# Two attention layers on TensorE: heads in pairs on the halves of the array, output with features on partitions

## The chip, the cores and the metric

The kernel runs on one core of one Trainium2 chip. The core has a matrix engine (TensorE, "PE"; its weight loads are shown apart as "PEld"), a vector engine (VectorE, "DVE"), a scalar engine (ScalarE, "ACT"), GpSimd ("POOL") and a queue for transfers (SyncE, "SP"). Each takes its instructions in order; they wait for each other by semaphores. The metric is the device time in microseconds, the median of several runs. Lower is better.

## What is computed

A hybrid network of four layers on a sequence of 256 tokens with 1024 features, in float32. Each layer is a SwiGLU block, a mixer and a second SwiGLU block, each followed by a weighted residual and a layer norm. The mixers are a state-space layer (layers 0 and 3), "fox" attention (layer 1: 16 heads of 64 features, causal, with a forget gate) and "moba" attention (layer 2, which for 256 tokens in one block of 256 is plain causal attention). What the change touches is, for each head:

```python
logits = einsum('bhqd,bhkd->bhqk', q, k) * 64 ** -0.5      # fox: + cum[q] - cum[k], summed log gates
logits = where(kpos <= qpos, logits, -inf)
p = softmax(logits, axis=-1)
o = einsum('bhqk,bhkd->bhqd', p, v)                         # then o @ w_out
```

## The kernel before, in words

The 256 tokens are two halves of 128, t = 0 and t = 1. All of a half's activations lie with its tokens on partitions, and are turned (features on partitions) by PE transposes to be a matmul's stationary operand. The weights are streamed once, in pieces of 128 x 2048 float32 (1 MB); each piece is split by ACT (`wh`, line 123) and DVE (`wl`, line 124) into two float32r parts, and every product with weights is three matmuls, high by high, high by low and low by high (lines 148 to 150). Half 1 follows half 0 by two pieces (`LAG`), so the two halves' work is interleaved, and a scheduler of the language that knows data dependencies and a cost of each instruction sets the final order on each engine.

An attention layer takes 16 pieces in the order of `ATT_ORDER`: for each of four groups of four heads one piece V (values) and two pieces Q (queries and keys), then four pieces O (the output projection, `down`). After a piece, stages are emitted by the table `post`. With q the second Q piece of group g:

- `stage_v` copies the values from PSUM to `kv`; `stage_q` (at q) copies queries and keys to SBUF (line 624), transposes them on PE, and writes the transposed queries, times 1/8, to `qz` (lines 627, 628) and the transposed keys to `kT` (line 629). After the transposes two heads lie on the two halves of the partitions, 64 features each. `qz` has a slot of 128 x 128 per head, whose other 64 partitions are zero: POOL cleared the tile (line 618). So a head's score matmul works on all 128 rows, and half of them meet zeros.
- `stage_s` (at q + 1) makes scores in a transposing bank `T()`: a bf16 matmul adds the causal mask (`mlo`, lines 643, 660), fox adds its gate rows by a selector (`sel`, line 654), and line 657 is queries by keys. t = 0 has 128 keys per head and all four heads in one bank; t = 1 has 256 keys (those of t = 0 and its own) and two heads per bank, one bank after the other. DVE takes the maximum of each row (line 662), ACT the exponential with its sum (line 667), DVE the reciprocal (line 670).
- `att` (at q + 2) transposes the probabilities on PE, copies them out (lines 687, 689) and multiplies: the transposed probabilities (128 keys x 128 queries) are stationary, 64 columns of values move (lines 695, 699, 700). The output has queries on partitions. DVE multiplies it by the reciprocals (line 702).
- `stage_a` (at q + 3) transposes that output on PE, two transposes of 128 columns, and splits it into `ah` and `al` for the output projection (`act_split`).

PSUM has two banks for `T()` (all transposes and scores), two for `G()` (the attention output among others) and four for accumulators. These matmuls of scores and values are in float32.

Of the kernel before, what the change touches and what calls it, by code (L numbers as in the profile page):

```python
# [49 lines left out]
def build(tc, x, wst, ln_g, ln_b, sm_dt, sm_rows, sm_conv, sm_nw, fx_f, fx_b, out, plan=None):  # L50
# [33 lines left out]
    K = {}  # L84
# [504 lines left out]
    def attn(st, kind, j):  # L589
# [27 lines left out]
        qz = spool.tile([128, 4, 128], F32, name="qz", tag="xD", bufs=2)  # L617
        nc.gpsimd.memset(qz, 0.0)
# [3 lines left out]
        def stage_q(g):  # L622
            qk = tmp(512, "t2", 4)
            nc.scalar.activation(qk, bank.pop(g), AF.Copy)
            tp = transposes(qk, 4).rearrange("p (a b) -> p a b", a=4)
            kT = kv[g][:, 0:256].rearrange("p (a b) -> p a b", a=2)
            nc.scalar.activation(qz[0:64, 0::2], tp[0:64, 0:2], AF.Copy, scale=0.125)
            nc.vector.tensor_scalar_mul(qz[64:128, 1::2], tp[64:128, 0:2], 0.125)
            nc.scalar.activation(kT, tp[:, 2:4], AF.Copy)
            if t == 0:  # L630
                s.kT[g] = kT

        def stage_s(g):
            kT = kv[g][:, 0:256].rearrange("p (a b) -> p a b", a=2)
            own = d.rows if fox else None
            rs = spool.tile([128, 12], F32, name="rs", bufs=4)
            nh = 4 if t == 0 else 2
            pt = []
            for b in range(4 // nh):
                tp = T()  # L640
                if t == 0:
                    Sv = tp.rearrange("p (h k) -> p h k", h=4)
                    nc.tensor.matmul(Sv, K["mlo"], rep4(4), start=True, stop=True, skip_group_check=True)
                    parts = [(kT, 0, own)]
                else:
                    Sv = tp.rearrange("p (h k) -> p h k", h=2)
                    parts = [(s.kT[g], 0, s.toend if fox else None), (kT, 128, own)]
                begun = t == 0
                for hh in range(nh):
                    h = b * nh + hh  # L650
                    for kt, off, rows in parts:
                        o = Sv[:, hh, off:off + 128]
                        if fox:
                            nc.tensor.matmul(o, sel(g * 4 + h), rows, start=not begun, stop=False,
                                             skip_group_check=True)
                            begun = True
                        nc.tensor.matmul(o, qz[:, h], kt[:, h // 2], start=not begun, stop=True, skip_group_check=True)  # L657
                        begun = True
                if t == 1:
                    nc.tensor.matmul(Sv[:, :, 128:256], K["mlo"], rep4(2), start=False, stop=True,  # L660
                                     skip_group_check=True)
                nc.vector.tensor_reduce(rs[:, b * nh:(b + 1) * nh], Sv, axis=AX.X, op=ALU.max, negate=True)
                p = tmp(512, "mt", 5)
                pv = p.rearrange("p (h k) -> p h k", h=nh)
                for hh in range(nh):
                    h = b * nh + hh
                    nc.scalar.activation(pv[:, hh], Sv[:, hh], AF.Exp, bias=rs[:, h:h + 1],
                                         accum_out=rs[:, 4 + h:5 + h])
                pt.append(p)
            nc.vector.reciprocal(rs[:, 8:12], rs[:, 4:8])  # L670
            ps_[g] = (pt, rs)
# [8 lines left out]
        def att(g):  # L680
            pt, rs = ps_.pop(g)
            pT = []
            for p in pt:
                tp = transposes(p, 4)
                e = tmp(512, "mt", 5)
                if t == 0:
                    nc.vector.tensor_copy(e, tp)
                else:
                    nc.scalar.activation(e, tp, AF.Copy)
                pT.append(e)  # L690
            o = G()
            for h in range(4):
                c64 = slice(h * 64, h * 64 + 64)
                if t == 0:
                    nc.tensor.matmul(o[:, c64], pT[0][:, h * 128:(h + 1) * 128], vs[g][:, c64], start=True, stop=True)
                else:
                    e = pT[h // 2]
                    b = (h % 2) * 256
                    nc.tensor.matmul(o[:, c64], e[:, b:b + 128], s.v[g][:, c64], start=True, stop=False)
                    nc.tensor.matmul(o[:, c64], e[:, b + 128:b + 256], vs[g][:, c64], start=False, stop=True)  # L700
            on = tmp(256, "t1", 5)
            nc.vector.tensor_mul(on.rearrange("p (a b) -> p a b", a=4),
                                 o[:, :256].rearrange("p (a b) -> p a b", a=4),
                                 rs[:, 8:12].unsqueeze(2).to_broadcast([128, 4, 64]))
            ons[g] = on

        ons = {}

        def stage_a(g):
            ahs[g] = act_split(ons.pop(g), 2)[0]  # L710
# [12 lines left out]
        for g in range(ATT_G):  # L723
# [5 lines left out]
            at(q + 3, stage_a, g)  # L729
# [201 lines left out]
```

## Time and profile before

| | |
|---|---|
| median of 3 runs | 2160.16 us (2158.58 to 2160.63) |
| profiled execution | 2158.25 us, its span 2156.1 us |
| PE busy | 2122.0 us (98%) |
| PEld busy | 1768.2 us (82%) |
| DVE busy | 1486.4 us (69%) |
| ACT busy | 1125.5 us (52%) |
| POOL busy | 477.6 us (22%) |

The span runs from the first to the last instruction of the profiled execution. Busy time of PE is a sum of records whose ends are modelled and which overlap in the pipe, so the spacing of starts says more than a record's length. A form such as "128\*128 128x64" gives the rows and columns of the array that a matmul uses, and then the operand that moves, as partitions x columns. The fox layer lies at about 757 to 897 us and the moba layer at about 1280 to 1403 us. "idle before <-" names what ended an engine's idle time.

### The profile page before, as it was taken

To read this page: it belongs to the slowest core of one execution; us is meant where nothing else is said; L and a number is where in the kernel's file an instruction comes from. 1 tells how busy PE (TensorE), PEld (TensorE's weight loads), DVE (VectorE), ACT (ScalarE), POOL (GpSimd) and SP (SyncE) were. 2 spreads that over 40 slices of the span, in tenths; PEclk is the share of its full clock that TensorE was granted. 3 is DMA by queue.
4 is the path that set the end of the run, shared out by engine and by line. 5 is a ranking of instruction groups with operands and counts; after the bars stand their busy time and mean duration, and the time that the engine had idled before them with its cause. 6 is when DMAs were issued, how large, how long until landed. Compare 5 with 4: busy or idle time off the path is not lost.

```text
span 2156.1 us, 29943 instructions
## 1 busy us (share of the span) xinstructions
PE 2122.0 (98%) x10370; PEld 1768.2 (82%) x10370; DVE 1486.4 (69%) x2959; ACT 1125.5 (52%) x2314; POOL 477.6 (22%) x862
## 2 busy tenths in 40 slices
PE   8999999999999999999999999999999999999998
PEld 6888878788888888888888888888888888788887
DVE  6657999855765674665575574666575679998655
ACT  6444776544444555444544455544454447665442
POOL 2331000233143200043233300033323310001431
PEclk9999999999999999999999999999999999999999
DMA  9775544676586643476666654376767665556772
GB/s 316 229 230 187 191 173 153 225 232 227 193 255 226 218 158 118 137 237 226 220 226 228 226 199 136 131 220 227 226 224 236 221 205 180 162 179 207 235 226 94
DMA packets 225927, 438.81 MB, mean 204 GB/s; under 512 B 20464, under 2 KB 20976, under 8 KB 225776
## 3 DMA queue, kind: packets, MB, share of 16 engines
q1 hardware_dynamic: 197616, 394.92, 55.1%
q0 software_dynamic: 28160, 41.99, 7.0%
q8 instruction: 81, 1.33, 0.3%
q14 instruction: 70, 0.57, 0.1%
HBM read 414.74 MB, written 22.09 MB: 203 GB/s over the span
## 4 chain that ended last, share of the span: by engine, by line
PE 93%; DVE 3%; ACT 1%; DMA 1%; issue 0%; POOL 0%; SPq 0%; DVEq 0%; ACTq 0%
PE gu L148 15%; PE gu L150 15%; PE gu L149 15%; PE acc L150 9%; PE acc L148 9%; PE acc L149 9%; PE ga L150 4%; PE ga L149 4%; PE ga L148 4%; PE tp L158 3%; PE gu L512 1%; DMA raw<-in_w_dram 1%; PE tp L657 1%; DVE wl L124 1%; DVE mt L502 1%
## 5 line engine op out<-in xcount | busy, mean ns | idle before, releaser
L124 DVE TENSOR_TENSOR wl<-raw,wh 128x512 fp32r<-128x512 f32 x1408 | 887.7, 683 | 361.8 <-ACT wh L123 360.2
L123 ACT ACTIVATE wh<-raw 128x512 fp32r<-128x512 f32 x1408 | 777.0, 621 | 528.0 <-PE gu L150 222.4
L148 PE MATMUL gu<-wh,xh 128*128 128x512 f32 (+1 forms) x1600 | 620.6, 388 | 7.1 <-ACT t L519 2.7
L150 PE MATMUL gu<-wh,xl 128*128 128x512 f32 (+1 forms) x1600 | 617.8, 387 | 0.9 <-DVE xl L124 0.9
L149 PE MATMUL gu<-wl,xh 128*128 128x512 f32 (+1 forms) x1600 | 617.4, 386 | 0.0
L246 POOL DMA_DIRECT2D aT<-turn x640 | 348.3, 551 | 503.4 <-issue 301.9
L148 PEld LDWEIGHTS gu<-wh,xh 128*128 128x128 f32 x1600 | 301.1, 188 | 69.7 <-ACT t L519 3.1
L150 PE MATMUL acc<-wh,al 128*128 128x512 f32 x896 | 353.5, 395 | 0.0
L149 PE MATMUL acc<-wl,ah 128*128 128x512 f32 x896 | 352.5, 393 | 0.0
L148 PE MATMUL acc<-wh,ah 128*128 128x512 f32 x896 | 351.5, 393 | 0.0
L150 PEld LDWEIGHTS gu<-wh,xl 128*128 128x128 f32 x1600 | 300.9, 188 | 61.6 <-DVE xl L124 2.1
L149 PEld LDWEIGHTS gu<-wl,xh 128*128 128x128 f32 x1600 | 301.2, 188 | 59.4 <-issue 0.5
L272 DVE TENSOR_TENSOR t<-t,gu 128x256 f32<-128x256 f32 x176 | 73.5, 418 | 192.5 <-ACT t L270 192.5
L270 ACT ACTIVATE t<-gu 128x256 f32<-128x256 f32 x176 | 67.5, 383 | 260.3 <-PE gu L150 239.5
L150 PEld LDWEIGHTS acc<-wh,al 128*128 128x128 f32 x896 | 168.4, 188 | 36.8 <-DVE al L124 1.9
L149 PEld LDWEIGHTS acc<-wl,ah 128*128 128x128 f32 x896 | 168.5, 188 | 34.4 <-issue 1.0
L148 PEld LDWEIGHTS acc<-wh,ah 128*128 128x128 f32 x896 | 168.5, 188 | 33.6
L148 PE MATMUL ga<-wh,xh 128*128 128x512 f32 (+1 forms) x448 | 159.6, 358 | 1.4 <-ACT xh L123 1.4
L242 POOL DMA_DIRECT2D turn<-tb x160 | 90.3, 565 | 318.6 <-DVE tb L240 297.7
L150 PE MATMUL ga<-wh,xl 128*128 128x512 f32 (+1 forms) x448 | 157.0, 351 | 0.1
L149 PE MATMUL ga<-wl,xh 128*128 128x512 f32 (+1 forms) x448 | 156.1, 349 | 0.0
L190 POOL TENSOR_TENSOR rstd<-ve,mhalf 128x1 f32<-128x1 f32 x24 | 22.6, 942 | 369.9 <-DVE ve L188 369.9
(179 smaller groups left out, 1707.0 us busy)
## 6 DMA issues: line engine op xcount, KB each, us to landing
raw<-in_w_dram SPq DMA_DIRECT2D x351, 1024.0 KB, 5.6
turn<-tb POOLq DMA_DIRECT2D x160, 128.0 KB, 3.4
aT<-turn POOLq DMA_DIRECT2D x640, 32.0 KB, 4.1
mt<-cums SPq DMA_DIRECT2D x32, 256.0 KB, 4.9
gb<-in_ln_g_dram SPq DMA_DIRECT2D x12, 512.0 KB, 4.6
gb<-in_ln_b_dram SPq DMA_DIRECT2D x12, 512.0 KB, 6.1
nw<-in_sm_nw_dram SPq DMA_DIRECT2D x8, 256.0 KB, 5.6
h<-in_x_dram SPq DMA_DIRECT2D x4, 256.0 KB, 4.3
```

What stands on the lines that cost most here:

```text
L123: a = nc.scalar.activation(wh, raw, AF.Copy)
L124: return a, nc.vector.tensor_sub(wl, raw, wh.bitcast(F32))
L148: nc.tensor.matmul(o, xh, wh, start=start, stop=False)
L149: nc.tensor.matmul(o, xh, wl, start=False, stop=False)
L150: nc.tensor.matmul(o, xl, wh, start=False, stop=stop)
L158: nc.tensor.transpose(tp[:, j * 128:(j + 1) * 128], src[:, j * 128:(j + 1) * 128], ident)
L190: nc.gpsimd.tensor_tensor(rstd, ve, mhalf, op=ALU.pow)
L242: nc.gpsimd.dma_start(dr, b.rearrange("p q k t -> p (q k t)"))
L246: nc.gpsimd.dma_start(aT[32 * q:32 * q + 32].rearrange("p i k t -> p i (k t)"), dv[q])
L270: nc.scalar.activation(sg, gu[:, :256], AF.Silu)
L272: nc.vector.tensor_mul(a, sg, gu[:, 256:])
L502: nc.vector.tensor_scalar(e[:, h], e[:, h], d.ncum[:, h0 + h:h0 + h + 1], 0.0, op0=ALU.add, op1=ALU.min)
```

## The change

- The queries are no longer padded: `qT` holds two pairs of heads, 128 partitions x 2 x 128, written by one DVE instruction. The cleared tile is gone. A head's score matmul takes 64 partitions, `qT[half, i]` by `kt[half, i]`, where half is rows 0 to 63 or 64 to 127; the two heads of a pair write to two banks, `Sv[0]` and `Sv[1]`, and follow each other in program order.
- Both banks are taken at the start for either half of the tokens. The mask comes first in each bank, then fox's selector matmuls, then all scores.
- The probabilities are multiplied by the reciprocals in SBUF, before they are transposed.
- In `att` the values, 128 keys x 64 features, are stationary and the transposed probabilities, 128 columns, move. A pair's outputs go to partitions 0 to 63 and 64 to 127 of one bank, so features are on partitions, and `ah` and `al` are split straight from PSUM. `stage_a` with its two transposes is gone. `h_at` gives a head's place in the order of t = 0, where the heads of a bank lie beside each other.

```diff
@@ -614,8 +614,7 @@
                 foxs[key].kT, foxs[key].v = {}, {}
             s = foxs[key]
         ahs, ps_, vs, kv = {}, {}, {}, {}
-        qz = spool.tile([128, 4, 128], F32, name="qz", tag="xD", bufs=2)
-        nc.gpsimd.memset(qz, 0.0)
+        qT = spool.tile([128, 2, 128], F32, name="qT", tag="xD", bufs=2)
 
         bank = {}
 
@@ -624,51 +623,48 @@
             nc.scalar.activation(qk, bank.pop(g), AF.Copy)
             tp = transposes(qk, 4).rearrange("p (a b) -> p a b", a=4)
             kT = kv[g][:, 0:256].rearrange("p (a b) -> p a b", a=2)
-            nc.scalar.activation(qz[0:64, 0::2], tp[0:64, 0:2], AF.Copy, scale=0.125)
-            nc.vector.tensor_scalar_mul(qz[64:128, 1::2], tp[64:128, 0:2], 0.125)
+            nc.vector.tensor_scalar_mul(qT, tp[:, 0:2], 0.125)
             nc.scalar.activation(kT, tp[:, 2:4], AF.Copy)
             if t == 0:
                 s.kT[g] = kT
 
         def stage_s(g):
+
             kT = kv[g][:, 0:256].rearrange("p (a b) -> p a b", a=2)
             own = d.rows if fox else None
             rs = spool.tile([128, 12], F32, name="rs", bufs=4)
-            nh = 4 if t == 0 else 2
-            pt = []
-            for b in range(4 // nh):
-                tp = T()
-                if t == 0:
-                    Sv = tp.rearrange("p (h k) -> p h k", h=4)
-                    nc.tensor.matmul(Sv, K["mlo"], rep4(4), start=True, stop=True, skip_group_check=True)
-                    parts = [(kT, 0, own)]
-                else:
-                    Sv = tp.rearrange("p (h k) -> p h k", h=2)
-                    parts = [(s.kT[g], 0, s.toend if fox else None), (kT, 128, own)]
-                begun = t == 0
-                for hh in range(nh):
-                    h = b * nh + hh
-                    for kt, off, rows in parts:
-                        o = Sv[:, hh, off:off + 128]
-                        if fox:
-                            nc.tensor.matmul(o, sel(g * 4 + h), rows, start=not begun, stop=False,
-                                             skip_group_check=True)
-                            begun = True
-                        nc.tensor.matmul(o, qz[:, h], kt[:, h // 2], start=not begun, stop=True, skip_group_check=True)
-                        begun = True
-                if t == 1:
-                    nc.tensor.matmul(Sv[:, :, 128:256], K["mlo"], rep4(2), start=False, stop=True,
-                                     skip_group_check=True)
-                nc.vector.tensor_reduce(rs[:, b * nh:(b + 1) * nh], Sv, axis=AX.X, op=ALU.max, negate=True)
-                p = tmp(512, "mt", 5)
+            parts = [(kT, 0, own)] if t == 0 else [(s.kT[g], 0, s.toend if fox else None), (kT, 128, own)]
+            nk = 128 * len(parts)
+            Sv = [T()[:, :2 * nk].rearrange("p (h k) -> p h k", h=2) for b in range(2)]
+            for b in range(2):
+                nc.tensor.matmul(Sv[b][:, :, nk - 128:nk], K["mlo"], rep4(2), start=True, stop=True,
+                                 skip_group_check=True)
+                if fox:
+                    for i in range(2):
+                        for kt, off, rows in parts:
+                            nc.tensor.matmul(Sv[b][:, i, off:off + 128], sel(g * 4 + 2 * i + b), rows, start=False,
+                                             stop=True, skip_group_check=True)
+            for i in range(2):
+                for kt, off, rows in parts:
+                    for b in range(2):
+                        half = slice(64 * b, 64 * b + 64)
+                        nc.tensor.matmul(Sv[b][:, i, off:off + 128], qT[half, i], kt[half, i], start=False, stop=True,
+                                         skip_group_check=True)
+            pt = [tmp(512, "mt", 5) for b in range(1 + t)]
+            for b in range(2):
+                nc.vector.tensor_reduce(rs[:, 2 * b:2 * b + 2], Sv[b], axis=AX.X, op=ALU.max, negate=True)
+                pv = pt[b if t else 0][:, 0 if t else b * 256:][:, :2 * nk].rearrange("p (h k) -> p h k", h=2)
+                for i in range(2):
+                    n = 2 * b + i
+                    nc.scalar.activation(pv[:, i], Sv[b][:, i], AF.Exp, bias=rs[:, n:n + 1],
+                                         accum_out=rs[:, 4 + n:5 + n])
+            nc.vector.reciprocal(rs[:, 8:12], rs[:, 4:8])
+            nh = 4 // (1 + t)
+            for n, p in enumerate(pt):
                 pv = p.rearrange("p (h k) -> p h k", h=nh)
-                for hh in range(nh):
-                    h = b * nh + hh
-                    nc.scalar.activation(pv[:, hh], Sv[:, hh], AF.Exp, bias=rs[:, h:h + 1],
-                                         accum_out=rs[:, 4 + h:5 + h])
-                pt.append(p)
-            nc.vector.reciprocal(rs[:, 8:12], rs[:, 4:8])
-            ps_[g] = (pt, rs)
+                nc.vector.tensor_mul(pv, pv, rs[:, 8 + n * nh:8 + (n + 1) * nh].unsqueeze(2).to_broadcast(
+                    [128, nh, nk]))
+            ps_[g] = pt
 
         def stage_v(g):
             kv[g] = tmp(512, "xe" if t == 0 and g % 2 else f"xdt{t}", 1 + t)
@@ -678,9 +674,9 @@
                 s.v[g] = vs[g]
 
         def att(g):
-            pt, rs = ps_.pop(g)
+
             pT = []
-            for p in pt:
+            for p in ps_.pop(g):
                 tp = transposes(p, 4)
                 e = tmp(512, "mt", 5)
                 if t == 0:
@@ -689,25 +685,22 @@
                     nc.scalar.activation(e, tp, AF.Copy)
                 pT.append(e)
             o = G()
-            for h in range(4):
-                c64 = slice(h * 64, h * 64 + 64)
-                if t == 0:
-                    nc.tensor.matmul(o[:, c64], pT[0][:, h * 128:(h + 1) * 128], vs[g][:, c64], start=True, stop=True)
-                else:
-                    e = pT[h // 2]
-                    b = (h % 2) * 256
-                    nc.tensor.matmul(o[:, c64], e[:, b:b + 128], s.v[g][:, c64], start=True, stop=False)
-                    nc.tensor.matmul(o[:, c64], e[:, b + 128:b + 256], vs[g][:, c64], start=False, stop=True)
-            on = tmp(256, "t1", 5)
-            nc.vector.tensor_mul(on.rearrange("p (a b) -> p a b", a=4),
-                                 o[:, :256].rearrange("p (a b) -> p a b", a=4),
-                                 rs[:, 8:12].unsqueeze(2).to_broadcast([128, 4, 64]))
-            ons[g] = on
-
-        ons = {}
-
-        def stage_a(g):
-            ahs[g] = act_split(ons.pop(g), 2)[0]
+            blocks = [vs[g]] if t == 0 else [s.v[g], vs[g]]
+            for i in range(2):
+                for kb, v in enumerate(blocks):
+                    for b in range(2):
+                        h = 2 * i + b
+                        e = pT[b][:, (2 * i + kb) * 128:] if t else pT[0][:, h_at(h) * 128:]
+                        nc.tensor.matmul(o[64 * b:64 * b + 64, i * 128:i * 128 + 128], v[:, h * 64:h * 64 + 64],
+                                         e[:, :128], start=kb == 0, stop=kb == len(blocks) - 1,
+                                         skip_group_check=True)
+            ah = spool.tile([128, 2, 128], FR, name="ah", bufs=5)
+            al = spool.tile([128, 2, 128], FR, name="al", bufs=5)
+            split(o[:, :256].rearrange("p (a b) -> p a b", a=2), ah, al)
+            ahs[g] = (ah, al)
+
+        def h_at(h):
+            return h % 2 * 2 + h // 2
 
         pieces, post = [], {}
 
@@ -726,7 +719,6 @@
             at(q + 1, stage_s, g)
             at(where["V", g, 0], stage_v, g)
             at(q + 2, att, g)
-            at(q + 3, stage_a, g)
         first_o = where["O", 0, 0]
         for i, (kind, g, n) in enumerate(pieces):
             if kind == "Q" and n == 0:
```

## Rows read from the trace of the kernel before

**Rows 1.** The page's busy times of each engine (us, share of the span, instructions), and the granted TensorE clock in 40 slices of the span, in tenths of full speed.

```profile
PE 2122.0 (98%) x10370; PEld 1768.2 (82%) x10370; DVE 1486.4 (69%) x2959; ACT 1125.5 (52%) x2314; POOL 477.6 (22%) x862
...
PEclk9999999999999999999999999999999999999999
```

**Rows 2.** The page's chain of work that ended last, shares of the span by engine.

```profile
PE 93%; DVE 3%; ACT 1%; DMA 1%; issue 0%; POOL 0%; SPq 0%; DVEq 0%; ACTq 0%
```

**Rows 3.** Busy time by stretch, for the two attention layers: the window, its length, then busy us (and instructions) of PE, PEld, DVE, ACT and POOL, the granted clock, the DMA share and GB/s.

```profile
757.00:895.00 138.00, 135.29 (x863) 117.19 (x861) 83.01 (x179) 71.57 (x190) 3.83 (x5) 1.00 0.42 138
1280.00:1403.00 123.00, 121.92 (x757) 105.18 (x757) 72.03 (x132) 69.99 (x178) 1.13 (x2) 1.00 0.43 147
```

**Rows 4.** Groups of instructions by line and form, whole execution: the two groups of score matmuls and the second value matmul of t = 1. Columns: count, then ns min/median/max, and the first and last start.

```profile
L657 PE MATMUL tp<-xdt,qz x128: 270/276/327, 784.5 to 1382.3; 128*128 128x128 f32 x128
...
L657 PE MATMUL tp<-xe,qz x64: 271/276/327, 810.4 to 1382.1; 128*128 128x128 f32 x64
...
L700 PE MATMUL gu<-xdt,mt x64: 274/276/276, 816.1 to 1391.1; 128*128 128x64 f32 x64
```

**Rows 5.** PE in order of time, a score block of t = 0 in moba (group 0) and the ordinary matmuls behind it. Columns: start us, us, engine, line, operation, out<-in, array, form, count.

```profile
1285.89 0.39 PE L643 MATMUL tp<-idb,mlo 128*128 128x512 bf16 x1
1286.11 1.06 PE L657 MATMUL tp<-xdt,qz 128*128 128x128 f32 x8
1286.92 0.47 PE L148 MATMUL ga<-wh,xh 128*128 128x512 f32 x1
1287.24 0.39 PE L149 MATMUL ga<-wl,xh 128*128 128x512 f32 x1
1287.46 0.39 PE L150 MATMUL ga<-wh,xl 128*128 128x512 f32 x1
```

**Rows 6.** The same view a little later: the four transposes of that group's probabilities, and its value block, each with the ordinary matmuls behind it.

```profile
1292.48 0.60 PE L158 MATMUL tp<-ident,mt 128*128 128x128 f32 x4
1292.83 0.48 PE L148 MATMUL ga<-wh,xh 128*128 128x512 f32 x1
1293.15 0.39 PE L149 MATMUL ga<-wl,xh 128*128 128x512 f32 x1
...
1294.77 1.00 PE L695 MATMUL gu<-xdt,mt 128*128 128x64 f32 x8
1295.57 0.48 PE L150 MATMUL ga<-wh,xl 128*128 128x512 f32 x1
1295.89 0.39 PE L148 MATMUL ga<-wh,xh 128*128 128x512 f32 x1
```

**Rows 7.** The same view in the state-space layer 0: a float32 matmul with 512 moving columns (two passes) and the ordinary matmuls behind it.

```profile
239.55 1.02 PE L489 MATMUL gu<-xe,t 128*128 128x512 f32 x2
240.01 0.79 PE L148 MATMUL ga<-wh,xh 128*128 128x512 f32 x1
240.64 0.40 PE L149 MATMUL ga<-wl,xh 128*128 128x512 f32 x1
```

**Rows 8.** PE in order of time in moba: the scores of t = 1 (first row, and the last mask behind them), the mask of the next block of t = 0, and the eight transposes of the probabilities of t = 1.

```profile
1329.48 0.38 PE L657 MATMUL tp<-xe,qz 128*128 128x128 f32 x2
...
1331.37 0.27 PE L660 MATMUL tp<-idb,mlo 128*128 128x256 bf16 x1
...
1334.35 0.39 PE L643 MATMUL tp<-idb,mlo 128*128 128x512 bf16 x1
...
1338.22 1.03 PE L158 MATMUL tp<-ident,mt 128*128 128x128 f32 x8
```

**Rows 9.** ACT in the same stretch: the last exponential of t = 1, and the last of t = 0.

```profile
1333.48 0.48 ACT L667 ACTIVATE mt<-tp,rs 128x256 f32<-128x256 f32 x1
...
1337.50 0.37 ACT L667 ACTIVATE mt<-tp,rs 128x128 f32<-128x128 f32 x1
```

**Rows 10.** DVE in the same stretch: the reciprocal of t = 1 and the reduction of t = 0 (in brackets the idle time before it).

```profile
1334.34 0.17 DVE L670 RECIPROCAL rs<-rs 128x4 f32<-128x4 f32 x1
1335.67 0.69 DVE L662 TENSOR_REDUCE rs<-tp 128x4 f32<-128x512 f32 x1 [1.16 <-PE tp L657]
```

**Rows 11.** Groups by line: the multiply of two SBUF tiles in the state-space layer (L504), and, in the attention layers, the row maximum (L662), the output's factor (L702), and the two copies of the queries (L627, L628). Columns as in rows 4; L627's row has busy us and mean ns instead, and the idle time before.

```profile
L504 DVE TENSOR_TENSOR mt<-mt,t x32: 678/684/693, 241.4 to 1940.2; 128x512 f32<-128x512 f32 x32
...
L662 DVE TENSOR_REDUCE rs<-tp x24: 680/691/694, 786.0 to 1383.2; 128x2 f32<-128x512 f32 x16, 128x4 f32<-128x512 f32 x8
...
L702 DVE TENSOR_TENSOR t<-gu,rs x16: 416/425/425, 795.0 to 1391.4; 128x256 f32<-128x256 f32 x16
...
L628 DVE TENSOR_SCALAR qz<-tp x16: 427/427/428, 776.5 to 1376.2; 64x256 f32<-64x256 f32 x16
...
L627 ACT ACTIVATE qz<-tp 64x256 f32<-64x256 f32 x16 | 6.0, 374 | 3.2 <-PE tp L158 3.1
```

**Rows 12.** Waits of the weight loads in the fox layer (750 to 910 us): line, what it waited for, total us, times, longest us.

```profile
PEld tp L158 <- ACT t L624: 3.2, 8, 1.1
```

## The prediction

> **What bounds the kernel now.** I read the page's busy times first. TensorE (PE) is busy 98% of the span, its weight loads (PEld) 82%, VectorE (DVE) 69% and ScalarE (ACT) 52%, and in the slices the granted clock never leaves full speed, 2.4 GHz [rows 1]. The chain of waits agrees: 93% of it is PE [rows 2]. So a microsecond matters where it is taken out of PE's queue, or where it makes that queue wait. The change touches two attention layers, layer 1 (fox) and layer 2 (moba). The windows around them hold 138 and 123 us, with PE busy 135.3 and 121.9 and DVE only 83.0 and 72.0 [rows 3]. Everything the change can give is inside these 261 us of 2156.
>
> Next, what one small matmul costs there. For 96 score matmuls the form view has 128 + 64 = 192 records [rows 4]: an fp32 matmul runs as two passes, each with a weight load. In a score block of moba the first of eight passes starts at 1286.11, and after them and one ordinary 512-column matmul the next starts at 1287.24: 1.13 us, less 0.23 us for the ordinary one (1287.24 to 1287.46) is 0.90, or 0.112 us a pass [rows 5]. Value passes take the same: 1294.77 to 1295.89 is 1.12 us for eight and one ordinary [rows 6]. Why the same, when scores stream 128 columns and values 64? An fp32 matmul with 512 moving columns shows the rate: 239.55 to 240.64 is 1.09 us for two passes and one ordinary matmul, so 0.43 us a pass, or 0.107 us per 128 columns and 0.054 per 64 [rows 7]. So a value pass is not held by its stream but by the load of its 128 stationary columns, and a score pass by both about equally. Nor do these blocks pay anything to enter or leave.
>
> **The change part by part.**
>
> *Scores.* A head has 64 features, and before, the other 64 rows met zeros. Now two heads stand on the row halves. If the halves run beside each other, and passes still start in program order, then head A's second pass shares its time with B's first, B's second with the next A's first, and so on: n pairs take 2n+1 slots of 0.112 us for 4n. Token half 0 (n = 2) goes from 8 slots to 5, half 1 (n = 4) from 16 to 9. Per group that is 10 slots, over 2 layers x 4 groups 80 slots: 9.0 us. From below: no overlap, nothing saved, since load and stream still want 0.107 each.
>
> *Values.* 96 matmuls, two passes each (L700 has 64 records for 32) [rows 4]. Now 64 columns of values are stationary and 128 weights stream: the load should halve, but the stream doubles to 0.107 us, so swapping by itself saves nothing. Two column halves side by side give the same 2n+1 of 4n: again 80 slots, 9.0 us, or nothing without overlap.
>
> *Transposes.* The output is born with features on partitions, so the two transposes per group and half go: 2 x 16 = 32 passes. Four transposes and an ordinary matmul take 1292.48 to 1293.15, so a pass costs (0.67 - 0.23)/4 = 0.11 us here too [rows 6], and 32 of them 3.6 us. This is sure.
>
> The gross gain is 9.0 + 9.0 + 3.6 = 21.6 us with overlap, 3.6 us without.
>
> *Changing the array's shape.* All passes before have shape 128*128; after, a score block is 64 rows high and a value block 64 columns wide, each between ordinary matmuls (the selector and mask matmuls of full height come first). That is in and out, twice, for 16 combinations of layer, half and group: 64 changes of shape. No row shows one. From below it is free, as entering a block is now. From above a whole matmul must end before the next load: its recorded 0.276 us [rows 4]. I take the record less the slot, 0.276 - 0.112 = 0.164 us, the time a matmul is in the pipe after the next would have started: one shape must leave the array before the other enters, but the load can be ready. 64 x 0.164 = 10.5 us (bounds 0 and 17.7).
>
> The Trainium skill, "TensorEngine Tiling (Array Packing)", Key Properties, speaks against the change here: changing the tiling mode, as opposed to the tile, drains the engine. By it the cost is not nothing; by [rows 5 and 6], with one mode only, entering a small block costs nothing. With the rule and my size the sum below is 8 us, without it 18.5. The same section says different tiles load and multiply in parallel; no run so far shows that.
>
> *PSUM banks.* There are two transpose banks (`T()`, two buffers). A score block of half 0 took one and now takes two; half 1 took them one after the other and now holds both until their exponentials are read. The masks of half 0 split in two, with the same columns. Where does PE reach a bank before it is free? In moba, half 0's mask starts at 1334.35 while half 1's last exponential runs 1333.48 to 1333.96; half 1's eight transposes start at 1338.22 while half 0's last exponential ends at 1337.87 [rows 8, 9]. The slack is about 0.4 us each time. With overlap and shape changes PE arrives earlier by 7 x 0.112 - 2 x 0.164 = 0.46 us, so the slack is about used up.
>
> *The softmax factor.* Before, DVE scaled the output (0.42 us, 16 times); now it scales the probabilities, 512 columns, 24 times. The nearest row is the same multiply in the SSM layer, 0.684 us [rows 11]. DVE also reduces half 0 in two pieces. It gains about 24 x 0.684 + 8 x (2 x 0.42 - 0.69) - 16 x 0.42 = 10.9 us over 261 us, where it has over 100 free. But this multiply stands before the transposes that PE needs next, and ahead of the next reduction: after the reciprocal at 1334.34 two multiplies reach to 1335.9, where now the reduction starts at 1335.67 [rows 10]. That takes 0.2 us from the same slack. What is queued behind it on DVE are weight splits, which run pieces ahead. I price banks and factor together at 0.19 us for each of 16 blocks, 3 us. Bounds: 0, if ordinary matmuls fill the hole, and 11 us, if one multiply per block is bare (16 x 0.684).
>
> *The query copy.* ACT loses 16 copies of 0.374 us and DVE's copy keeps its price, 64 or 128 partitions high [rows 11]; POOL loses a memset. The weight loads wait 3.2 us in the fox window for the copy that comes before it [rows 12], and that one stays. I count zero; less than nothing, up to a tenth of a microsecond per group, is possible. The split of the output reads PSUM directly: the same two operations, a multiply fewer, and nobody waits. Its `G()` bank is held for two operations, not one, and is asked for again only at the other half's next value block, a piece later; if that cover were gone it would cost one DVE operation of 256 columns, 0.42 us, per block, or 7 us.
>
> **Sum.** 2158.25 (the profiled execution; its span is 2156.1) - 21.6 + 10.5 + 3 = 2150.2. The median of the runs is 2160.16, 1.9 above it, so I forecast 2152 for the median.
>
> **Rivals.**
>
> *Free changes of shape.* The halves overlap and no drain shows: 2160.2 - 21.6 + 3 = 2142. For it: mixing 256- and 512-column and fp32 passes costs nothing now. Against: those all use the whole array.
>
> *The whole price.* Overlap, but each change waits for the matmul's end and a bare load, 17.7 us, and the stall of 3: 2160.2 - 21.6 + 17.7 + 3 = 2159, no change that can be told.
>
> *No overlap (slower).* The place is the two-pass fp32 matmul in the score and value blocks: two passes of one head, each with its load, come before the other head, and if a load of the second half cannot run beside the first half's, nothing is shared. Then 2160.2 - 3.6 + 10.5 + 3 = 2170. It decides against the change as soon as a shape change costs more than about (3.6 - 3)/64 = 0.01 us. For it: loads in all rows come in one line, 0.11 us apart even where the stream is half as long [rows 6]. Against: those all load the same rows of the array.
>
> *It does not do what it says.* No overlap and no price of shape: the transposes alone, 2160.2 - 3.6 + 3 = 2160.
>
> **How the numbers follow.** Forecast 0.42, free changes 0.16, the whole price 0.18, no overlap 0.18, only the transposes 0.06. A measurement tells no change from one over 0.2%, 4.3 us: faster is below 2155.8, slower above 2164.5. The forecast and the free case give faster 0.58; the whole price and the transposes alone give the same, 0.24, of which 0.02 may scatter over the upper bound; with the case of no overlap that leaves 0.22 for the same and 0.20 for slower. The range runs from just under the free case to just short of the no-overlap case, 2141 to 2169; the forecast's own range, with stalls from 0 to 6 us and shape changes from 0.1 to 0.22 us each, is 2145 to 2159.
>
> **What will show it.** In the profile after, a score block of half 0 should run from its first pass to the next ordinary matmul in about 5 x 0.112 + 2 x 0.164 = 0.9 us, half 1 in 9 x 0.112 + 2 x 0.164 = 1.3 us (now 0.9 [rows 5], and 1329.48 to 1331.37 with a mask between [rows 8]), with records of shape 64*128 whose starts are closer than 0.1 us. If they stay 0.11 apart, overlap is wrong; if the gap to the ordinary matmul behind a block is the usual, the price of shape is. Waits of PE for ACT's exponentials or for DVE's new multiply, over 3 us in sum in the two windows, would show the banks and the factor mis-sized. The transposes of the output must be gone: 32 fewer. A time above 2159 makes the forecast wrong, as does one below 2145.

## The result

The changed kernel takes 2148.39 us, the median of four runs (2147.68 to 2148.70), against 2160.39 for the kernel before beside it: a ratio of 0.9945, interval 0.9932 to 0.9957, or 12.0 us faster. The profiled execution went from 2158.25 to 2147.68 us, 10.6 us faster; the forecast for it was 8.1 faster.

The page of the profile after, busy times and chain of waits:

```profile
PE 2111.0 (98%) x10346; PEld 1745.7 (81%) x10346; DVE 1493.1 (70%) x2975; ACT 1121.4 (52%) x2298; POOL 476.0 (22%) x858
...
PE 91%; DVE 4%; ACT 2%; DMA 1%; issue 1%; POOL 0%; DVEq 0%; SPq 0%; ACTq 0%
```

PE lost 11.0 us of busy time [rows 1] and is still what bounds the kernel. The starts of the 24 layer-norm instructions on POOL (L190) date the gain: up to the fox layer the two traces differ by 0.2 to 0.5 us, from the eighth to the tenth start (the fox layer) the difference grows by 5.3, from the fourteenth to the sixteenth (moba) by 4.7, and after that it moves by no more than 0.3.

The shape of the work changed as the diff says. PE in order of time after the change, moba, group 0: masks, the scores of half 0 and the ordinary matmuls behind them; then its value block; then the scores of half 1.

```profile
1280.24 0.39 PE L640 MATMUL tp<-idb,mlo 128*128 128x256 bf16 x2
1280.57 0.71 PE L651 MATMUL tp<-xdt,qT 64*128 64x128 f32 x8
1281.21 0.50 PE L148 MATMUL ga<-wh,xh 128*128 128x512 f32 x1
1281.55 0.40 PE L149 MATMUL ga<-wl,xh 128*128 128x512 f32 x1
1281.78 0.39 PE L150 MATMUL ga<-wh,xl 128*128 128x512 f32 x1
...
1289.16 0.66 PE L694 MATMUL gu<-mt,xdt 128*64 128x128 f32 x8
1289.75 0.50 PE L150 MATMUL ga<-wh,xl 128*128 128x512 f32 x1
1290.09 0.40 PE L148 MATMUL ga<-wh,xh 128*128 128x512 f32 x1
...
1297.51 0.39 PE L640 MATMUL tp<-idb,mlo 128*128 128x256 bf16 x2
1297.83 1.16 PE L651 MATMUL tp<-xdt,qT 64*128 64x128 f32 x16
1298.92 0.39 PE L148 MATMUL ga<-wh,xh 128*128 128x256 f32 x1
1299.15 0.28 PE L149 MATMUL ga<-wl,xh 128*128 128x256 f32 x1
```

Read a block from its first start to the ordinary matmul's: sixteen score passes take 1.09 us where eight took 0.81 [rows 5]. But a block now pays at its edges. From the masks at 1280.24 to 1281.55 are 1.31 us; less 0.23 for the ordinary matmul, 0.22 for two masks and 0.45 for four slots of 0.112, 0.41 us is left. It lies in three places: 0.10 us before the first pass (0.33 us for two masks that take 0.22), 0.10 us behind the first pair of passes, and 0.20 us on leaving (0.09 before the ordinary matmul and 0.11 behind it, 0.34 where 0.23 is usual). Before the change that ordinary matmul took 0.32 as well [rows 5], but it started 0.03 us behind the last pass; from the last pass to the start after it were 0.34 us then and are 0.54 now, so the 0.20 stands. So the eight passes of half 0 save almost nothing, 0.86 us for 0.90; the sixteen of half 1 save about 0.5.

The weight loads' own records say more of these edges. The loads of the score block of half 0 and of the ordinary matmul behind it, first in the kernel before (the block of [rows 5]), then after the change:

```profile
1285.89 1.09 PEld L657 LDWEIGHTS tp<-xdt,qz 128*128 128x128 f32 x8
1286.89 0.19 PEld L148 LDWEIGHTS ga<-wh,xh 128*128 128x128 f32 x1
...
1280.56 0.52 PEld L651 LDWEIGHTS tp<-xdt,qT 64*128 64x128 f32 x8 [0.21 <-issue]
1281.21 0.19 PEld L148 LDWEIGHTS ga<-wh,xh 128*128 128x128 f32 x1
```

Before, a block's first load started 0.22 us ahead of its pass (1285.89, and 1286.11 in [rows 5]). After the change it starts 2 ns ahead of it, and so does the first load behind a block; in this trace that is so at every entry into a score or value block and at every exit. "Issue" means that the profile names nothing that the load waited for. So no load ran ahead across a change of shape, and the 0.10 us behind the first pair and the 0.11 behind the first ordinary matmul are about one load's slot (0.11 us by the value passes before the change [rows 6]). Read so, a change costs about 0.20 us, half of it before its first load and half behind it; into a value block it costs 0.14 (0.09 and 0.05), and its loads have 64 columns instead of 128. That the second half is this load alone is worked out from these starts and not tested by itself.

The value block of half 1 in group 1, the same view:

```profile
1332.37 0.40 PE L149 MATMUL ga<-wl,xh 128*128 128x512 f32 x1
1332.69 0.43 PE L694 MATMUL gu<-mt,xe 128*64 128x128 f32 x2
1333.06 0.50 PE L150 MATMUL ga<-wh,xl 128*128 128x512 f32 x1
1333.49 0.32 PE L694 MATMUL gu<-mt,xe 128*64 128x128 f32 x1
1333.49 0.32 PE L694 MATMUL gu<-mt,xdt 128*64 128x128 f32 x1
1333.65 0.27 PE L694 MATMUL gu<-mt,xe 128*64 128x128 f32 x1
...
1334.51 0.50 PE L148 MATMUL ga<-wh,xh 128*128 128x512 f32 x1
```

Two things are to be seen. Passes on the two halves do start together (1333.49 twice). And the block is cut: one matmul (two passes) goes at 1332.69, an ordinary matmul follows, and only then the other fourteen passes, so the block enters and leaves its shape twice, and the first matmul has nobody beside it. The ordinary matmul in between takes 0.43 us to the next start (1333.06 to 1333.49), where 0.23 is usual.

The bank wait, the same view some microseconds earlier, and then the two lists of PE's waits (fox window, moba window), of which one line each names that wait:

```profile
1326.76 0.28 PE L640 MATMUL tp<-idb,mlo 128*128 128x256 bf16 x1
1327.54 0.27 PE L640 MATMUL tp<-idb,mlo 128*128 128x256 bf16 x1 [0.49 <-ACT mt L659]
1327.74 0.71 PE L651 MATMUL tp<-xdt,qT 64*128 64x128 f32 x8
...
PE tp L640 <- ACT mt L659: 1.2, 3, 0.5
...
PE tp L640 <- ACT mt L659: 1.5, 3, 0.6
```

Half 0's second mask stands until ACT has read the last scores of half 1 from that bank: six times, 2.7 us.

One wait went away that nobody had counted. The same lists of the kernel before have, in either layer, the first line below, which the lists of after don't have. The other two show its place in fox, the last output transpose and the matmul that waits:

```profile
PE gu L148 <- ACT xh L123: 1.1, 1, 1.1
...
899.81 0.27 PE L158 MATMUL tp<-ident,t 128*128 128x128 f32 x1
901.15 0.50 PE L148 MATMUL gu<-wh,xh 128*128 128x512 f32 x1 [1.07 <-ACT xh L123]
```

The line is there again in "scores only" and absent in "values only" (both below), so it goes with the output's transposes. At each layer's end PE had run out of work: the last output of half 1 was still being transposed and split, so its output projection could not fill the time in which the next block's input was transposed.

To sum PE's queue over both layers I add, from the trace, the time from each PE start to the next by kind, between the layer-norm marks named above (us):

| | before | after | values only | late half first | both | halves apart |
|---|---|---|---|---|---|---|
| score blocks (mask, selector, scores) | 29.1 | 27.6 | 29.1 | 27.6 | 25.2 | 39.0 |
| value blocks | 21.7 | 16.2 | 13.6 | 13.4 | 13.4 | 15.9 |
| transposes of queries, keys and output | 13.1 | 8.0 | 8.0 | 8.0 | 8.0 | 8.0 |
| ordinary matmuls | 191.5 | 192.7 | 190.5 | 191.2 | 189.8 | 191.8 |
| both layers, mark to mark | 272.3 | 262.4 | 258.9 | 258.2 | 254.4 | 272.2 |

The last four columns are experiments, below. The score blocks, which fill half of the diff, gave 1.5 us, the value blocks 5.5 and the transposes 5.1, of which 2.1 are the wait at the two layers' ends, since it stands behind a transpose. Ordinary matmuls cost 1.2 more: those inside a cut value block alone are seven of 0.43 us where 0.23 is usual, 1.4 us.

### The profile page after: what moved, and what is told of

The parts are those of the page before. It is cut to its first block, busy times and chain, and to the rows that moved or that the text cites. A ratio compares the mean times of both kernels' runs of the same rounds, so it can differ in the third digit from the quotient of the medians.

```text
span 2145.9 us, 29868 instructions
## 1 busy us (share of the span) xinstructions
PE 2111.0 (98%) x10346; PEld 1745.7 (81%) x10346; DVE 1493.1 (70%) x2975; ACT 1121.4 (52%) x2298; POOL 476.0 (22%) x858
## 4 chain that ended last, share of the span: by engine, by line
PE 91%; DVE 4%; ACT 2%; DMA 1%; issue 1%; POOL 0%; DVEq 0%; SPq 0%; ACTq 0%
PE gu L150 16%; PE gu L148 16%; PE gu L149 15%; PE acc L150 9%; PE acc L148 9%; PE acc L149 9%; PE ga L148 4%; PE ga L149 3%; PE ga L150 3%; PE tp L158 3%; DVE wl L124 1%; PE gu L512 1%; DMA raw<-in_w_dram 1%; PE gu L694 1%; DVE mt L502 1%
## 5 line engine op out<-in xcount | busy, mean ns | idle before, releaser
L270 ACT ACTIVATE t<-gu 128x256 f32<-128x256 f32 x176 | 67.7, 384 | 258.9 <-PE gu L150 241.1
L190 POOL TENSOR_TENSOR rstd<-ve,mhalf 128x1 f32<-128x1 f32 x24 | 22.6, 942 | 481.5 <-DVE ve L188 481.5
```

Source lines behind the costliest of these rows:

```text
L190: nc.gpsimd.tensor_tensor(rstd, ve, mhalf, op=ALU.pow)
L270: nc.scalar.activation(sg, gu[:, :256], AF.Silu)
```

## The experiments

Medians are of the runs named; the kernel before ran beside each, at 2159.7 to 2160.4. "After" is 2148.4. An interval reaches about 2.7 us to either side, and execution times also move by 2 us before the first of the two layers (its first mark lies at 766.1 to 768.4 us in these traces). So where two versions lie less than 4 us apart, the sum of the two layers, mark to mark, is given too: it holds the edit's work and little else.

**Order of the halves, scores.**

```diff
-            for i in range(2):
-                for kt, off, rows in parts:
-                    for b in range(2):
+            for b in range(2):
+                for i in range(2):
+                    for kt, off, rows in parts:
```

> Only the order of the score matmuls changes: all of one row half, then all of the other, so that neighbours stand on the same rows. Theory (the row halves run side by side): a block of n pairs goes from 2n slots of 0.112 us plus about 0.1 us back to 4n slots, 1.1 us more per group, 8 groups: 9 us slower than the change, about 2157 us, and starts 0.11 us apart. Rival (halves do not help each other; the gain comes from the missing transposes and the shorter queue): no difference, 2148 us.

Measured 2149.54 (2149.09 to 2149.84), ratio to before 0.9950 (0.9936 to 0.9965): 1 us, not 9 (263.0 us in the layers, for 262.4). Taken alone it looks like the rival. The trace says otherwise; a score block of half 0 and one of half 1 in this kernel:

```profile
1281.99 0.72 PE L651 MATMUL tp<-xdt,qT 64*128 64x128 f32 x8
1282.64 0.50 PE L148 MATMUL ga<-wh,xh 128*128 128x512 f32 x1
...
1299.26 1.71 PE L651 MATMUL tp<-xdt,qT 64*128 64x128 f32 x16
1300.90 0.39 PE L148 MATMUL ga<-wh,xh 128*128 128x256 f32 x1
```

Half 0 takes 0.65 us as in the change: with four passes of the one half in front of four of the other the passes were paired all the same, starts 13 ns apart. Half 1, eight in front of eight, takes 1.64 us for 1.09. In its starts the second half's first pass begins 6 ns behind the first half's fifth, four places in front of it, as in half 0. So the order in the kernel's text doesn't bind over a short distance, and the experiment didn't take away what it meant to. Whether PE started passes out of their order or the scheduler had changed the order, the trace doesn't tell. The half 1 blocks cost 8 x 0.55 = 4.4 us more, and 3.8 of it came back, 2.2 of that since PE reached the banks later and the waits for them shrank from 2.7 to 0.5 us. A better experiment was needed, and follows as "halves apart".

**Order of the halves, values.** The same exchange of loops in `att`.

> Only the order of the value matmuls changes: all of one column half, then all of the other. Theory (column halves run side by side): 4n slots for 2n again, 0.9 to 1.1 us per group, 7 to 9 us slower than the change, about 2156 us. Rival (a value pass became cheaper because its load has 64 columns, with or without a neighbour): no difference, 2148 us.

Measured 2148.63 (2147.69 to 2149.35), ratio 0.9946 (0.9931 to 0.9961), no difference (262.9 us in the layers for 262.4). The value blocks of half 0 were paired in spite of the order, as above. Those of half 1 lost part of the sharing but were no longer cut, since one half's values need only the first copied tile, and the two came out even: 17.9 us of value blocks for 16.2, ordinary matmuls 191.7 for 192.7. The median decides nothing, but the trace does. A value block of half 1:

```profile
1308.25 1.58 PE L694 MATMUL gu<-mt,xdt 128*64 128x128 f32 x16
1309.76 0.50 PE L150 MATMUL ga<-wh,xl 128*128 128x512 f32 x1
```

The first and the last four of its sixteen starts stand alone, 0.109 us apart (0.16 between the first two), and only the middle is shared: 1.51 us. Sixteen passes paired throughout take 1.02 (the block under "both mends"). So the column halves run side by side, and a load of 64 columns alone doesn't make a pass cheaper.

**Values only.** Scores as before the change, values as after it; the probabilities of half 1 lie in the order of before, so the index in `att` follows.

```diff
-        qT = spool.tile([128, 2, 128], F32, name="qT", tag="xD", bufs=2)
+        qz = spool.tile([128, 4, 128], F32, name="qz", tag="xD", bufs=2)
+        nc.gpsimd.memset(qz, 0.0)
...
-                        e = pT[b][:, (2 * i + kb) * 128:] if t else pT[0][:, h_at(h) * 128:]
+                        e = pT[i][:, (2 * b + kb) * 128:] if t else pT[0][:, h * 128:]
```

> Scores as before the change (zero-padded queries, 128 rows, banks one by one), values as after it, with the factor on the probabilities. If the score side nets what its matmuls saved less its shape changes alone (9.0 - 5.2 us), this is 4 us slower than the change, 2152. If the bank waits and the gaps before the first score eat most of that, under 2 us: 2149 to 2150.

Measured 2145.72 (2144.22 to 2147.85), ratio 0.9934 (0.9919 to 0.9948): faster than the whole change by 2.7 us (258.9 us in the layers for 262.4), outside both expectations. The table shows why: without the new scores the value blocks fall from 16.2 to 13.6 us and the ordinary matmuls from 192.7 to 190.5, more than the old scores add (29.1 for 27.6). The old order puts both heads of the first pair into the tile that is copied first, so the block isn't cut. The new scores put a pair's heads into two banks, hence into two tiles, and the first pair waits for the second copy.

**Scores only.** Scores as after, values as before, with the factor on the output and its transposes.

```diff
-            at(q + 2, att, g)
+            at(q + 2, att, g)
+            at(q + 3, stage_a, g)
```

> Scores as after the change, values as before it (probabilities stationary, output scaled and transposed). The value side with its transposes should then be worth most of the gain: by PE's starts 5.5 us in the value blocks and 5.1 us in the transposes, so 2158 to 2159. Rival (forecast's sizes, 3.8 and 3.6 us): 2156.

Measured 2158.74 (2156.61 to 2159.34), ratio 0.9993 (0.9984 to 1.0003). The new scores by themselves can't be told from no change, as expected (271.8 us in the layers for 272.3: what the score blocks gain, 1.5 us, the ordinary matmuls lose); the value side with its transposes carries the gain, 10 us.

**Late half first.**

```diff
-                    for b in range(2):
+                    for b in (1, 0):
```

> In the value block the second column half of each pair comes first, so that the block of token half 1 starts with the probabilities that are copied last. Theory (the block is cut after its first matmul because only the first copy is there, and that costs two more shape changes and an unshared start, 0.43 us, 8 times): 3 us faster than the change, 2145. Rival (PE only waits for the later copy instead): no difference, 2148.

Measured 2145.57 (2144.19 to 2146.20), ratio 0.9933 (0.9919 to 0.9946): 2.8 us faster than the change, as the theory had it (258.2 us in the layers for 262.4). The block is whole:

```profile
1331.28 0.44 PE L694 MATMUL gu<-mt,xe 128*64 128x128 f32 x4
1331.55 0.39 PE L694 MATMUL gu<-mt,xdt 128*64 128x128 f32 x4
1331.77 0.39 PE L694 MATMUL gu<-mt,xe 128*64 128x128 f32 x4
1331.99 0.39 PE L694 MATMUL gu<-mt,xdt 128*64 128x128 f32 x4
```

**Another bank.** Half 0's second scores go to the pair of banks of the attention output.

```diff
-            Sv = [T()[:, :2 * nk].rearrange("p (h k) -> p h k", h=2) for b in range(2)]
+            Sv = [(G if b and t == 0 else T)()[:, :2 * nk].rearrange("p (h k) -> p h k", h=2) for b in range(2)]
```

> Token half 0 takes its second score bank from the pair that holds the attention output, not from the transposing pair. Theory (PE's 2.7 us of waits at the second mask are for that bank): 2 to 3 us faster than the change, 2146. Rival (the wait moves to the output bank or to the exponentials anyway): no difference or slower.

Measured 2145.70 (2144.47 to 2148.01), ratio 0.9934 (0.9921 to 0.9946): 2.7 us faster (258.6 us in the layers for 262.4). PE's wait for the exponentials at a mask fell from 2.7 us to this, and is absent in moba:

```profile
PE tp L640 <- ACT mt L659: 0.2, 1, 0.2
```

**No factor.** The probabilities are not divided by their sum: 24 DVE multiplies are left out.

> The softmax factor is left out altogether (the probabilities are not divided by their sum), which takes away 24 DVE multiplies of 512 columns. Theory (DVE has room; PE waits almost nowhere for that multiply): within 0.5 us of the change, 2148. Rival (the factor holds back the reductions of the next scores and so the banks): 2 us or more faster.

Measured 2148.22 (2147.63 to 2148.88), ratio 0.9945 (0.9933 to 0.9958), no difference from the change (262.2 us in the layers for 262.4). The multiply that moved from 256 to 512 columns costs nothing that can be told.

**More shape changes.** Each score block is cut in two by its masks.

```diff
+            for i in range(2):
+                for b in range(2):
+                    nc.tensor.matmul(Sv[b][:, i, nk - 128:nk], K["mlo"], K["idb"], start=True, stop=True,
+                                     skip_group_check=True)
...
+                for kt, off, rows in parts:
+                    for b in range(2):
```

> Each score block is cut in two by its masks and selectors: mask and scores of the first pair of heads, then of the second. That adds 32 shape changes and 16 starts of a block, and leaves the work the same. Theory: 32 x 0.15 us plus 16 x 0.1 us for the unshared first load, 6 us slower than the change, 2155. Rival (shape changes are free and the gaps at a block come from semaphores): under 1 us.

Measured 2152.51 (2151.40 to 2154.44), ratio 0.9967 (0.9955 to 0.9980): 4.1 us slower than the change, not under 1. In the two layers it is 4.8 us (267.2 for 262.4). A cut block of half 0:

```profile
1284.31 0.29 PE L641 MATMUL tp<-idb,mlo 128*128 128x128 bf16 x2
1284.53 0.49 PE L650 MATMUL tp<-xdt,qT 64*128 64x128 f32 x4
1284.95 0.29 PE L641 MATMUL tp<-idb,mlo 128*128 128x128 bf16 x2
1285.17 0.49 PE L650 MATMUL tp<-xdt,qT 64*128 64x128 f32 x4
```

Two slots, 0.22 us, take 0.42 from the first pass to the next mask. The waits for banks are smaller here again (0.9 us in the fox list for 1.2, 0.2 in the moba list for 1.5). With those 1.6 us added to the 4.8, an estimate, the cut costs 6.4 us, which is 32 x 0.20.

**Halves apart.** The mask and selectors of the second bank stand between the scores of the two row halves; shape changes are as many as in the run before.

```diff
+            for b in range(2):
+                half = slice(64 * b, 64 * b + 64)
+                nc.tensor.matmul(Sv[b][:, :, nk - 128:nk], K["mlo"], rep4(2), start=True, stop=True,
+                                 skip_group_check=True)
...
+                for i in range(2):
+                    for kt, off, rows in parts:
+                        nc.tensor.matmul(Sv[b][:, i, off:off + 128], qT[half, i], kt[half, i], start=False, stop=True,
```

> In each score block the mask and the selectors of the second bank stand between the scores of the two row halves, so that no score matmul has a neighbour on the other half. Shape changes are as many as in the run with the blocks cut in two (32 more than the change). Theory (the row halves run side by side, also where the program order puts them apart by a few passes): 96 slots of 0.112 us more than that run, less 2 or 3 us of bank waits that the slower PE no longer meets: 8 to 11 us slower, 2160 to 2163. Rival (no overlap, so nothing to lose): as that run, 2152 to 2153.

Measured 2159.55 (2157.53 to 2160.76), ratio 0.9995 (0.9986 to 1.0004): 7.0 us above the cut blocks, 11.2 above the change, somewhat below the range of the theory and far from the rival. The two layers alone are 5.0 us above the cut blocks (272.2 for 267.2): the blocks of half 1 in moba, masks included, take 2.60 us for 1.72, eight slots more, as the theory has it, but half 0's blocks no longer wait for a bank. A block of half 1:

```profile
1305.06 0.28 PE L641 MATMUL tp<-idb,mlo 128*128 128x256 bf16 x1
1305.28 1.16 PE L650 MATMUL tp<-xdt,qT 64*128 64x128 f32 x8
1306.36 0.28 PE L641 MATMUL tp<-idb,mlo 128*128 128x256 bf16 x1
1306.58 1.16 PE L650 MATMUL tp<-xdt,qT 64*128 64x128 f32 x8
```

Eight passes with nobody on the other half take 1.08 us; sixteen with the halves paired took 1.09 after the change. That is the overlap of the row halves, shown.

**Both mends.** Late half first, and another bank.

> The late column half first in the value blocks and the other bank for half 0's second scores, together. Theory (two separate losses, 2.8 and 2.7 us by the single runs): 2143 us. Rival (the time won at the one place is waited for at the other): 2145 to 2146, no better than either alone.

Measured 2140.88 (2140.18 to 2141.72), ratio to before 0.9908 (0.9893 to 0.9923): 19.5 us below the kernel before, 7.5 below the change, more than the sum of the two, 5.5. A score block of half 0 and a value block of half 1:

```profile
1300.14 0.28 PE L640 MATMUL tp<-idb,mlo 128*128 128x256 bf16 x1
1300.27 0.27 PE L640 MATMUL gu<-idb,mlo 128*128 128x256 bf16 x1
1300.47 0.37 PE L651 MATMUL tp<-xe,qT 64*128 64x128 f32 x1
1300.47 0.37 PE L651 MATMUL gu<-xe,qT 64*128 64x128 f32 x1
...
1305.87 1.09 PE L694 MATMUL gu<-mt,xdt 128*64 128x128 f32 x16
1306.89 0.50 PE L149 MATMUL ga<-wl,xh 128*128 128x512 f32 x1
```

The second mask follows the first without a wait, and sixteen value passes run as one block in 1.02 us. This is the fastest version of the study.

**Half 0 as before.** Half 0 makes its scores in the old way, half 1 in the new; late half first.

```diff
-            at(q + 1, stage_s, g)
+            at(q + 1, stage_s if t else stage_s0, g)
```

> Token half 0 makes its scores as before the change (zero-padded, one bank), half 1 as after it; the late column half comes first. Theory (half 0's two pairs save in passes about what their shape changes and starts cost, and their second bank costs a wait): 2 to 3 us faster than the run with the late half first alone, about 2143. Rival (half 0's pairs pay for themselves): slower than that run, 2147 or more.

Measured 2142.94 (2141.99 to 2144.81), ratio 0.9919 (0.9906 to 0.9933): 2.6 us faster than late half first alone, as expected (256.1 us in the layers for 258.2). Pairing half 0's scores on two of the transposing banks cost more than it gave. With another bank for them (2140.88) it is at least no loss.

## Why the prediction was right

- *Overlap of the halves*: right, shown for the row halves by "halves apart" and for the column halves by the trace of the values' order. The rivals without overlap fall. What the Trainium skill, "TensorEngine Tiling (Array Packing)", Key Properties, says of tiles that work in parallel agrees: sixteen paired score passes take 1.09 us, eight alone 1.08. The forecast's picture of it was wrong: it had 2n+1 slots for n pairs, the +1 from a stagger of passes. The trace has no stagger, passes of the two halves start 5 to 8 ns apart and n pairs take 2n slots. The odd 0.1 us behind the first pair (0.05 in value blocks) is an edge.
- *Price of a shape change*: not free, as forecast; "more shape changes" confirms it. But the step "the load can be ready" failed: the first load never starts ahead of its pass across a change. A change costs about 0.20 us, 0.14 into a value block, for 0.164 forecast. The two slips cancel: a score block was to pay 2 x 0.164 + 0.112 = 0.44 us above its 2n slots, and pays 0.41. That the blocks last what was forecast, 0.86 us for 0.9 and 1.30 for 1.3, is luck in this part. The rival of the whole price had the bare load right and the size, 0.276 each, wrong. The sentence of the Trainium skill, "TensorEngine Tiling (Array Packing)", Key Properties, that changing the tiling mode drains the engine agrees with the 0.09 to 0.10 us before each first load; the load behind it is not in that sentence.
- *Number of shape changes*: wrong. I counted 64 and took the blocks as whole. The trace has 88, 17 entries into a score shape, 27 into a value shape, and as many exits. Half 1's eight value blocks are cut, which makes 16 more and with the unshared first matmul costs 2.8 us by the medians and 4.1 in the layers ("late half first"); the rest are mostly in the last blocks of the layers, where transposes of the next block's input come in between.
- *Banks and factor*, 3 us: the sum was right by luck, its parts were not. The banks cost 2.7 us ("another bank"; 3.8 in the layers), the factor nothing that can be told ("no factor"). The slack of 0.4 us read from [rows 8 and 9] was indeed used up.
- *Transposes*, "this is sure", 3.6 us: mis-sized. PE's queue gave 5.1, 3.0 of it passes and 2.1 waiting that went with them, 1.1 us at each layer's end. I had looked at the waits inside the layers and had not followed the output's transposes into the last output piece.
- *Sum*: the forecast for the profiled execution was 8.1 faster, measured 10.6, so the direction and the range are right, and the size is in part a balance of errors. The layer ends (2 us more) and the cut blocks (3 to 4 us less) stand against each other; the rest is spread over terms too small to separate here.
- *Parts*: the forecast gave scores and values the same worth, 9.0 - 5.2 us each, and took the bank waits off at the end. The runs put nearly all of the gain on the value side; the score side's saving is eaten by its own edges, its bank and the cut that it causes in the values.

What stays open: whether the pairing over four passes is PE's doing or the scheduler's, and why both mends together give 7.5 us where singly they give 5.5. In the layers by the trace they give 7.9 together, and 4.1 and 3.8 singly, which adds up; so the single medians may simply lie a little high.

## What to carry to other kernels

Pairing small matmuls on halves of the array halves their slots, but each block of such matmuls pays a few tenths of a microsecond at its edges (0.4 here, 0.2 for each change of shape): it pays where a block is long and whole, so order the operands such that the block starts with the one that comes last. Count the PSUM banks that the pair takes at once, and who reads them last. And follow a removed step to the end of its stage: a wait there can be worth as much as the step.

## What the runs showed of the hardware that was not expected

Matmuls on different halves of the array start within 4 to 14 ns of each other even where the kernel's text puts four passes of one half in front of the other (score blocks of half 0 in the first experiment), and not where it puts eight: there only the middle of the block was shared (1.64 us for 1.09). No weight load started ahead of its pass across a change of the array's shape (2 ns, where 0.22 us was usual at a score block in moba before), and a change cost about 0.20 us. And a value pass with 64 stationary and 128 moving columns, alone on its half, keeps the slot of 0.11 us (starts 0.109 us apart at the head of half 1's value blocks in the second experiment): half the load doesn't help while the stream has 128 columns.
